# Low weight parts of the side-by-side steps made on GpSimd instead of stored and reloaded, weight sums moved, keys evacuated first, zero matmuls at the start

## The chip, the cores and the metric

The kernel runs on one core of one Trainium2 chip. The metric is the device time of one execution in microseconds (us); the median of three runs is given. TensorE is called PE, VectorE DVE, ScalarE ACT, GpSimd POOL; SyncE (SP) issues the DMAs.

## What is computed

One decoder layer on x of 2048 rows (tokens) by 2048 columns, in float32. One input projection feeds a convolution branch (1024 channels) and a sliding-window attention (16 heads of 64, 2 key/value heads); both are gated, joined and mapped by an output projection, and the result is added to the scaled input and normalized.

```python
proj = x @ w_in + b_in                       # 2048 x 2048 by 2048 x 5376
c_val, c_glu, c_gate, q, k, v, a_gate = split(proj)
h = causal_depthwise_conv(c_val * sigmoid(c_glu), width=31) + conv_b
y_conv = silu(layer_norm(h)) * silu(c_gate)
y_attn = window_attention_with_sinks(q, k, v) * silu(a_gate)
y = concat(y_conv, y_attn) @ w_out + b_out
out = layer_norm(2 ** 0.25 * x + y)
```

## The kernel before, in words

**Split products.** Every float32 matrix product is made of three matmuls. A matrix is split into a high part (rounded to the matmul's own type by a copy on ACT) and a low part (the rest: the matrix minus the high part, by `lo_part`, L134, one subtraction on DVE or POOL). `mm3` (L783) then adds high x high, high x low and low x high into one PSUM bank. A weight tile is 128 x 1024; its raw, high and low form (`wr`, `wh`, `wl`) have three buffers each.

**Steps.** The work is a list of steps (L664), one weight tile of 24 matmuls each. The input projection takes four chunks of 512 tokens, each of 52 steps (`PER`):

- eight `first` steps: four column tiles (k, v, one value and one gate tile of the convolution) side by side in four banks, each step adding two of the sixteen pieces of the inner dimension;
- 36 `in` steps: the 18 column tiles 4 to 21 one by one, two steps a tile. Beside them runs the attention of the chunk (`att_scores`, `att_transpose`, `att_values`, from step 13 of the chunk);
- eight `last` steps: the tiles 22 to 25 side by side, as in `first`.

Then the gates (`gate`) and the output projection (`out`) follow, both as Strassen products with seven products instead of eight, in eight steps each.

**Low parts of the weights.** In chunk 0 the low part of each of the 52 weight tiles is computed (on DVE for `first`, on POOL otherwise; `split_w`, L717) and stored to DRAM (`wlo`, L571, stored at L894). In chunks 1 to 3 `load_lo` (L711) loads it back two steps ahead; `has_lo` (L704) tells which steps have a stored low part.

**Weight sums.** The Strassen products need sums of weight quarters (`tsum`) and, for every other piece, stored low parts (`olo`). They are made in 32 jobs beside the projection: `tsum_load` (L580) loads four tiles of 128 x 512, `tsum_part` (L590) makes up to four subtractions (L598) and, for even pieces, seven high copies on ACT and seven low parts, on POOL, and queues their stores. Job j starts at step 10 + 6 j (L772).

**Background.** `run_bg` (L175) runs four or five pieces a step of the depthwise convolution on DVE (31 taps of 128 x 512 a tile, L234), or of its norm. The sums over channels (`csum`, L239, and `vsum`, L276) run on POOL.

**Evacuation.** At the end of the `first` steps `evac_in` (L377) empties four banks, in the order 2, 3, 1, 0 (L914): the two convolution tiles, v, then k. For k, the last block of the chunk before is first copied to the front of the key tiles (L390 and 391). The next step's tile takes the bank that k had.

**What sets the order.** All DMAs go through one queue on SP, in the order in which they are written (`dma`, L71). Each engine runs its instructions in one fixed order, made when the program is built, from priorities in the source's order and from modelled readiness; an instruction that waits holds back all behind it on its engine.

At the start (L851 to 866) the first weights and inputs are loaded and split, and PE begins when they are there.

Of the kernel before, what the change touches and what calls it, by code (L numbers as in the profile page):

```python
# [8 lines left out]
F32 = mybir.dt.float32  # L9
# [7 lines left out]
P = 128  # L17
# [11 lines left out]
NB = SC // P  # L29
KT = D // P  # L30
NSLOT = 69

PRODS = {"gate": (1, 2, 5, 6, 3, 7, 4), "out": (1, 2, 6, 5, 3, 7, 4)}

# [16 lines left out]
def hybrid_layer_kernel(ctx, tc, x, xT, w_first, w_in, w_out, consts, b_out, ln_g, ln_b, out):  # L51
# [79 lines left out]
    def copy(dst, src):  # L131
        A.activation(out=dst, in_=src, func=AF.Copy)  # L132
# [244 lines left out]
    def evac_in(c, t, kind, j, ps):  # L377
# [9 lines left out]
            store_later(hd[j][:, 30 + c * SC:30 + c * SC + SC], u)  # L387
            later.append((st["n"] + 3, lambda: cq.append((c, j))))
        elif kind == "k":
            for t in (*ks, *kl):  # L390
                copy(t[:, 0:P], t[:, 4 * P:5 * P].bitcast(F32))
            for kv in range(2):
                rows = slice(kv * HD, (kv + 1) * HD)
                for dst in (rows, slice((1 - kv) * HD, (2 - kv) * HD)):
# [3 lines left out]
        elif kind == "q":  # L398

            st["q", j] = [slot(f"q{kv}_{c}_{j}", F32R) for kv in range(2)]  # L400
            for kv in range(2):
                qs = st["q", j][kv]
                rows, other = slice(kv * HD, (kv + 1) * HD), slice((1 - kv) * HD, (2 - kv) * HD)
                A.activation(out=qs[rows], in_=ps[rows], func=AF.Identity, bias=b1[rows])
                V.scalar_tensor_tensor(out=qs[other], in0=ps[rows], scalar=b1[rows], in1=qs[rows].bitcast(F32),
                                       op0=ALU.add, op1=ALU.subtract)
        elif kind == "v":
            raw = slot(f"vraw{c}")
            A.activation(out=raw, in_=ps, func=AF.Identity, bias=b1)
            copy(vt[:, 0], vt[:, 4].bitcast(F32))  # L410
            pt = ps_pt.tile([P, 4, P], F32, tag="pt", name=f"vT{c}")
            for b in range(NB):
                T.transpose(out=pt[:, b, :], in_=raw[:, b * P:(b + 1) * P], identity=ident)
            for kv in range(2):
                src = pt[:, :, kv * HD:(kv + 1) * HD]
                hi, lo = vt[:, 1:5, kv, 0:HD], vt[:, 1:5, kv, HD:P]
                copy(hi, src)
                V.tensor_tensor(out=lo, in0=src, in1=hi.bitcast(F32), op=ALU.subtract)
# [130 lines left out]
    def gen_y(what, blk, i, k):  # L549
# [8 lines left out]
        if i == 5:  # L558
# [9 lines left out]
            for i in (5, 6, 7, 4) for q in pieces}  # L568
    olo = {(i, *q): dram.tile([P, 1024], F32, tag=f"O{i}_{q}", name=f"O{i}_{q[0]}{q[1]}_{q[2]}")
           for i in range(1, 8) for q in pieces if q[2] % 2 == 0}  # L570
    wlo = [dram.tile([P, 1024], F32, tag=f"wlo{n}", name=f"wlo{n}") for n in range(52)]  # L571

    def quarter(what, dp, p, a, b):

# [88 lines left out]
    PER = 52  # L663
# [38 lines left out]
                yield  # L702

    def has_lo(n):  # L704
        return n >= PER and (steps[n][0] not in strassen or steps[n][4] % 2 == 0)

    def lo_src(n):
        s = steps[n]
# [8 lines left out]
    def split_w(n, parts=1):  # L717
# [6 lines left out]
        for i in range(parts):  # L724
            w = slice(i * 1024 // parts, (i + 1) * 1024 // parts)
            copy(hi[:, w], t[:, w])
            if not has_lo(n):
                lo_part(G if steps[n][0] != "first" else V, lo[:, w], t[:, w], hi[:, w])
        los[n] = lo
        splits[n] = ((hi[:, 0:512], hi[:, 512:1024]), (lo[:, 0:512], lo[:, 512:1024]))  # L730

# [37 lines left out]
                    at(base + 47 + p, gen_y, *prods[0], k)  # L769
    for j in range(32):  # L770
        job = (("gate", "out")[j // 16], j // 8 % 2, j // 2 % 4, j % 2)
        n = 10 + 6 * j  # L772
        at(n, tsum_load, *job)
        for k, i in enumerate((1, 2, 3, 5, 7, 6, 4)):
            at(n + 2 + k // 2, tsum_part, *job, i)
# [72 lines left out]
            store(c, s, d)  # L848


    w0 = load_w(0, 2)  # L851
    load_x(0, 0)
    next(w0)
# [14 lines left out]
    for n, s in enumerate(steps):  # L868
# [20 lines left out]
        else:  # L889
            list(load_w(n + 3))  # L890
            load_lo(n + 2)
            split_w(n + 2)
        if n < PER:
            dma(out=wlo[n], in_=los[n].bitcast(F32))  # L894
        for f, *args in att.get(n, []):
            f(*args)
        if s[0] in ("first", "last"):
# [13 lines left out]
                        h, l = (w[t // 2][:, t % 2 * 256 + kk * P:t % 2 * 256 + kk * P + P] for w in (hi, lo))  # L911
                    mm3(st["acc"][t], h, l, xh, xl, k == 0, k == KT - 1)
            if p == 7 and s[0] == "first":
                for t in (2, 3, 1, 0):  # L914
                    evac_in(c, t, *ORDER[t], st["acc"][t])
            elif p == 7:
                for t in range(4):
                    evac_in(c, 22 + t, *ORDER[22 + t], st["acc"][t])
            run_bg(5)
        elif s[0] == "in":  # L920
            _, c, t, kind, j, hf = s
# [145 lines left out]
```

## Time and profile before

| | us |
|---|---|
| median of three runs (lowest, highest) | 2650.05 (2649.9, 2653.05) |
| the profiled execution | 2651.39 |
| its span, first to last instruction | 2649.7 |
| PE busy | 2547.9 (96%) |
| DVE busy | 2086.1 (79%) |
| ACT busy | 1303.0 (49%) |
| POOL busy | 972.9 (37%) |
| mean granted TensorE clock | 0.988 of full speed |

The profile lists what each engine did in one execution. "Busy" of PE is from modelled ends of matmuls, which overlap; the distance from one start to the next tells the pace. In the list of waits, a row such as `PE in L786 <- DMA wl<-wlo` says that the matmuls of line 786 on tile `in` waited for the DMA that loads `wl` from `wlo`, with the total, the number of times and the longest in us. A group row gives engine, operation, tiles, shapes and count, then busy us and mean ns, then the idle time before. A row of the timeline gives start and duration in us, and in brackets the idle time before and what ended it. A row of a window gives busy us and count of each engine, the granted clock, the DMA share and GB/s.

### The profile page before, as it was taken

What the parts mean: (1) busy time and instruction counts of PE and PEld (TensorE: products, weight loads), DVE (VectorE), ACT (ScalarE), POOL (GpSimd) and SP (SyncE); (2) the same over time, 40 slices, a digit from 0 to 9 for tenths busy, and PEclk for the clock granted to TensorE, in tenths of its full rate; (3) what the DMA queues carried; (4) which work ended last, traced back from release to release, by engine and by line L of the source; (5) the groups of instructions that cost most, each with busy time, mean ns of one, the idle gap of its engine ahead of it and who ended that gap; (6) DMA issues with size and microseconds to landing.
All of it is one profiled execution on the core that took longest, in us unless ns stands there. A gap on an engine that the chain in (4) does not pass through costs nothing.

```text
span 2649.7 us, 35489 instructions
## 1 busy us (share of the span) xinstructions
PE 2547.9 (96%) x11680; PEld 2108.7 (80%) x11680; DVE 2086.1 (79%) x3261; ACT 1303.0 (49%) x2461; POOL 972.9 (37%) x614
## 2 busy tenths in 40 slices
PE   8999989999899999999999999999999999999995
PEld 6788777887688887888887787888888888888884
DVE  3787798858887868889759999977775677987688
ACT  4577435776347765467535434544554323233321
POOL 2677824445144452426423222324222222212224
PEclk9999999999999999999999999999999999999997
DMA  7675898757986689966887767786888987899794
GB/s 278 217 260 193 287 326 277 243 177 262 339 299 249 203 296 350 328 226 224 272 274 248 246 236 268 268 292 216 292 289 289 327 304 267 305 357 341 276 319 156
DMA packets 331674, 720.43 MB, mean 272 GB/s; under 512 B 37857, under 2 KB 95329, under 8 KB 331489
## 3 DMA queue, kind: packets, MB, share of 16 engines
q1 hardware_dynamic: 331488, 718.16, 78.4%
q8 instruction: 92, 1.51, 0.2%
q14 instruction: 94, 0.76, 0.1%
HBM read 564.79 MB, written 153.21 MB: 271 GB/s over the span
## 4 chain that ended last, share of the span: by engine, by line
PE 60%; DVE 18%; DMA 9%; ACT 5%; issue 3%; POOL 2%; SPq 2%; DVEq 0%; ACTq 0%; POOLq 0%
PE in L786 6%; DVE cv L234 6%; PE in L785 6%; PE in L784 6%; PE out L785 3%; PE out L784 3%; PE out L786 3%; SPq L75 2%; PE gate_s L786 2%; PE gate_s L784 2%; PE gate_s L785 2%; DMA wl<-wlo 2%; PE out_s L784 2%; PE out_s L786 2%; PE out_s L785 2%
## 5 line engine op out<-in xcount | busy, mean ns | idle before, releaser
L135 POOL TENSOR_TENSOR wl<-wr,wh 128x1024 fp32r<-128x1024 f32 (+1 forms) x158 | 393.8, 2494 | 973.7 <-ACT wh L132 639.6
L132 ACT ACTIVATE wh<-wr 128x1024 fp32r<-128x1024 f32 (+1 forms) x436 | 455.0, 1046 | 546.5 <-DMA wr<-in_w_in_dram 81.4
L234 DVE SCALAR_TENSOR_TENSOR cv<-h,cst,cv 128x512 f32<-128x512 f32 x928 | 696.0, 752 | 18.8
L786 PE MATMUL in<-xh,wl 128*128 128x512 f32 x1280 | 502.1, 393 | 14.0 <-DMA wl<-wlo 14.0
L784 PE MATMUL in<-xh,wh 128*128 128x512 f32 x1280 | 504.1, 394 | 9.7 <-ACT xh L132 6.2
L785 PE MATMUL in<-xl,wh 128*128 128x512 f32 x1280 | 502.9, 393 | 0.0
L786 PEld LDWEIGHTS in<-xh,wl 128*128 128x128 f32 x1280 | 242.6, 190 | 67.6 <-DMA wl<-wlo 17.3
L784 PEld LDWEIGHTS in<-xh,wh 128*128 128x128 f32 x1280 | 242.5, 189 | 59.7 <-ACT xh L132 6.9
L785 PEld LDWEIGHTS in<-xl,wh 128*128 128x128 f32 x1280 | 242.4, 189 | 49.1 <-DVE xl L135 1.0
L785 PE MATMUL out<-wl,yhout 128*128 128x512 f32 x448 | 175.5, 392 | 6.4 <-DMA wl<-O_out 5.5
L132 ACT ACTIVATE yhout<-yrout 128x512 fp32r<-128x512 f32 x112 | 70.0, 627 | 216.3 <-DVE yrout L557 206.7
L786 PE MATMUL out<-wh,ylout 128*128 128x512 f32 x448 | 175.1, 391 | 0.0
L784 PE MATMUL out<-wh,yhout 128*128 128x512 f32 x448 | 166.9, 391 | 0.4 <-ACT wh L132 0.4
L135 POOL TENSOR_TENSOR plc<-pmc,phc 128x512 fp32r<-128x512 f32 x64 | 83.2, 1299 | 223.9 <-ACT phc L132 186.4
L135 DVE TENSOR_TENSOR ylgate<-yrgate,yhgate 128x512 fp32r<-128x512 f32 x112 | 109.7, 980 | 40.0 <-ACT yhgate L132 39.5
L135 DVE TENSOR_TENSOR ylout<-yrout,yhout 128x512 fp32r<-128x512 f32 x112 | 102.1, 912 | 45.0 <-ACT yhout L132 43.8
L322 ACT ACTIVATE pr<-pr,sm 128x128 f32<-128x128 f32 x256 | 99.6, 390 | 66.1 <-DVE sm L318 65.8
L132 ACT ACTIVATE yhgate<-yrgate 128x512 fp32r<-128x512 f32 x112 | 69.9, 625 | 115.3 <-DVE yrgate L557 93.9
L784 PE MATMUL gate_s<-yhgate,wh 128*128 128x512 f32 x304 | 119.0, 391 | 2.1 <-DVE g L451 1.9
L786 PE MATMUL gate_s<-yhgate,wl 128*128 128x512 f32 x304 | 119.1, 392 | 1.9 <-POOL wl L135 1.9
L785 PE MATMUL gate_s<-ylgate,wh 128*128 128x512 f32 x304 | 118.6, 390 | 0.0
L784 PE MATMUL gate<-yhgate,wh 128*128 128x512 f32 x288 | 112.8, 392 | 0.2 <-DVE g L451 0.2
(368 smaller groups left out, 5872.2 us busy)
## 6 DMA issues: line engine op xcount, KB each, us to landing
wl<-wlo SPq DMA_DIRECT2D x156, 512.0 KB, 5.1
wr<-in_w_in_dram SPq DMA_DIRECT2D x144, 512.0 KB, 5.9
yrout<-yd SPq DMA_DIRECT2D x192, 256.0 KB, 5.8
wr<-in_w_in_dram SPq DMA_DIRECT2D x320, 128.0 KB, 4.4
yrgate<-in_xT_dram SPq DMA_DIRECT2D x144, 256.0 KB, 5.1
wr<-T_gate SPq DMA_DIRECT2D x64, 512.0 KB, 6.3
wr<-T_out SPq DMA_DIRECT2D x61, 512.0 KB, 6.9
wl<-O_gate SPq DMA_DIRECT2D x56, 512.0 KB, 3.9
```

Source lines behind the costliest of these rows:

```text
L75: queue.append(nc.sync.dma_start(out=out, in_=in_).ins)
L132: A.activation(out=dst, in_=src, func=AF.Copy)
L135: eng.tensor_tensor(out=dst, in0=src, in1=hi.bitcast(F32), op=ALU.subtract)
L234: V.scalar_tensor_tensor(out=a if t == TAPS - 1 else acc, in0=x_, scalar=w, in1=acc, op0=ALU.mult, op1=ALU.add)
L322: A.activation(out=p3[:, u, :], in_=p3[:, u, :], func=AF.Exp, scale=HD ** -0.5, bias=sm[:, 1, u:u + 1], accum_out=sm[:, 3, u:u + 1])
L784: T.matmul(o, lh, mh, start=start, stop=False)
L785: T.matmul(o, lh, ml, start=False, stop=False)
L786: T.matmul(o, ll, mh, start=False, stop=stop)
```

## The change

- **Low parts.** Only the 36 `in` steps (8 to 43 of a chunk) keep stored low parts. In the `first` and `last` steps of chunks 1 to 3 the low part is computed on POOL from the raw tile and the high part. In chunk 0 the `first` steps still use DVE; the 16 side-by-side steps no longer store theirs.
- **Weight sums.** Jobs 0 to 7 stay where they were; in chunks 1 to 3 eight jobs a chunk start at steps 8, 12, 17, 21, 26, 30, 35 and 39 of the chunk.
- **Evacuation.** The order is 0, 1, 2, 3: k, v, then the convolution's tiles. The copies from the chunk before (keys and values) move from the evacuation to step 4 of the `first` steps.
- **Zero matmuls.** DVE clears one tile, and ten matmuls of it into a bank that is otherwise unused then stand ahead of everything on PE.

```diff
+WARM = 10
...
         elif kind == "k":
-            for t in (*ks, *kl):
-                copy(t[:, 0:P], t[:, 4 * P:5 * P].bitcast(F32))
...
             A.activation(out=raw, in_=ps, func=AF.Identity, bias=b1)
-            copy(vt[:, 0], vt[:, 4].bitcast(F32))
...
-    wlo = [dram.tile([P, 1024], F32, tag=f"wlo{n}", name=f"wlo{n}") for n in range(52)]
+    wlo = {n: dram.tile([P, 1024], F32, tag=f"wlo{n}", name=f"wlo{n}") for n in range(8, 44)}
...
     def has_lo(n):
-        return n >= PER and (steps[n][0] not in strassen or steps[n][4] % 2 == 0)
+        kind = steps[n][0]
+        return n >= PER if kind == "in" else kind in strassen and steps[n][4] % 2 == 0
...
             if not has_lo(n):
-                lo_part(G if steps[n][0] != "first" else V, lo[:, w], t[:, w], hi[:, w])
+                lo_part(V if n < 8 else G, lo[:, w], t[:, w], hi[:, w])
...
-        n = 10 + 6 * j
+        n = 10 + 6 * j if j < 8 else j // 8 * PER + 8 + j % 8 * 9 // 2
...
+    warm = slot("warm", F32R)
+    V.memset(warm.bitcast(F32), 0.0)
+    wps = right_banks("warm")[3]
+    for k in range(WARM):
+        T.matmul(wps, warm[:, 0:P], warm, start=k == 0, stop=k == WARM - 1)
...
-        if n < PER:
+        if n in wlo:
             dma(out=wlo[n], in_=los[n].bitcast(F32))
...
             if p == 7 and s[0] == "first":
-                for t in (2, 3, 1, 0):
+                for t in range(4):
                     evac_in(c, t, *ORDER[t], st["acc"][t])
...
+            if p == 4 and s[0] == "first":
+                for t in (*ks, *kl):
+                    copy(t[:, 0:P], t[:, 4 * P:5 * P].bitcast(F32))
+                copy(vt[:, 0], vt[:, 4].bitcast(F32))
```

## The prediction

> **What bounds the kernel now.** I read the page first, then busy time by stage, then the list of waits of PE.
>
> ```profile
> span 2649.7 us, 35489 instructions
> PE 2547.9 (96%) x11680; PEld 2108.7 (80%) x11680; DVE 2086.1 (79%) x3261; ACT 1303.0 (49%) x2461; POOL 972.9 (37%) x614
> ```
>
> PE is the bound, so only time in which PE stands still or runs slowly can be won. To see where that is, I counted 24 matmuls a step along PE, cut the projection where the eight side-by-side steps at a chunk's start and end begin and stop (192 matmuls), and asked for busy time between the cuts (busy us and count by engine, granted clock, DMA share, GB/s).
>
> ```profile
> core 0: us, PE busy (x) PEld busy (x) DVE busy (x) ACT busy (x) POOL busy (x), PEclk, DMA share, GB/s
> 0.00:56.20 56.20, 48.02 (x192) 37.94 (x192) 22.34 (x31) 26.85 (x40) 9.42 (x22) 1.00 0.79 276
> 56.20:304.10 247.90, 238.67 (x1188) 201.45 (x1189) 174.82 (x308) 153.92 (x382) 185.68 (x115) 0.99 0.71 236
> 304.10:348.40 44.30, 43.88 (x194) 35.90 (x193) 41.99 (x56) 14.59 (x19) 31.31 (x18) 1.00 0.91 311
> 348.40:403.50 55.10, 47.08 (x194) 37.28 (x192) 52.53 (x72) 19.56 (x25) 9.22 (x6) 0.94 0.91 309
> 403.50:659.10 255.60, 242.21 (x1193) 202.99 (x1194) 197.41 (x367) 174.36 (x414) 124.14 (x94) 0.98 0.70 239
> 659.10:710.00 50.90, 46.23 (x193) 36.87 (x192) 36.72 (x50) 14.40 (x18) 11.84 (x9) 0.97 0.98 334
> 710.00:757.90 47.90, 44.61 (x194) 35.67 (x192) 41.48 (x59) 22.57 (x31) 15.14 (x12) 1.00 0.86 315
> 757.90:997.20 239.30, 235.84 (x1191) 199.61 (x1192) 186.25 (x355) 158.62 (x390) 114.07 (x89) 1.00 0.74 259
> 997.20:1041.20 44.00, 44.00 (x196) 36.40 (x195) 39.04 (x63) 24.96 (x35) 5.97 (x5) 1.00 1.00 338
> 1041.20:1090.30 49.10, 45.78 (x193) 36.91 (x192) 41.33 (x59) 24.04 (x35) 26.20 (x20) 0.97 0.99 365
> 1330.10:1374.20 44.10, 44.10 (x196) 36.46 (x196) 30.46 (x42) 16.57 (x23) 3.68 (x2) 1.00 0.83 276
> ```
>
> The same 192 matmuls take 44.00 us where nothing is waited for (997.2 to 1041.2). I take that as the floor of such a stage. Over it lie 11.1 us in the first steps of chunk 1, 6.9 in its last steps, 3.9 in the first of chunk 2, 0 in its last, 5.1 in the first of chunk 3 and 0.1 in its last: **27.1 us in the six stages that lose their loads of low parts**. Their DMA share is 0.83 to 1.00, that of the long single-tile stages 0.70 to 0.74. The waits say what it is:
>
> ```profile
> PE in L786 <- DMA wl<-wlo: 14.0, 7, 3.6
> PE in1l_s L786 <- DMA wl<-wlo: 4.7, 4, 3.0
> PE in L784 <- DVE kl L396: 3.5, 4, 2.0
> PE gate_s L786 <- POOL wl L135: 1.9, 1, 1.9
> PE vT L413 <- ACT vraw L409: 1.4, 1, 1.4
> PE in0l_s L786 <- POOL wl L135: 0.4, 1, 0.4
> ```
>
> Eleven waits for a stored low part make 18.7 us (columns: total, times, longest). Much of the rest is a slow clock behind a wait:
>
> ```profile
> 669.30:672.70 3.40, 3.40 (x9) 2.65 (x8) 3.22 (x6) 0.00 (x0) 0.00 (x0) 0.51 1.07 389
> 1495.40:1498.80 3.40, 3.40 (x9) 2.32 (x8) 2.67 (x5) 3.30 (x7) 0.00 (x0) 0.50 0.92 311
> ```
>
> At a granted clock of 0.51, 9 matmuls ran where 15 fit at the 0.227 us that a matmul takes at full clock (below). That is 1.4 us a stretch.
>
> **The change part by part.**
>
> *Low parts by POOL.* 48 loads and 16 stores go, out of these:
>
> ```profile
> wl<-wlo SPq DMA_DIRECT2D x156, 512.0 KB, 5.1
> wlo<-wl SPq DMA_DIRECT2D x52, 512.0 KB, 5.8
> L135 POOL TENSOR_TENSOR wl<-wr,wh 128x1024 fp32r<-128x1024 f32 x154 | 387.4, 2516 | 971.4 <-ACT wh L132 637.3 <-DMA wr<-in_w_in_dram 100.8 <-DMA wl<-O_out 62.6
> L598 POOL TENSOR_TENSOR tbgate<-tbgate,tbgate 128x512 f32<-128x512 f32 x64 | 86.0, 1344 | 58.4 <-DMA tbgate<-in_w_in_dram 51.7 <-PE in L786 3.8
> L135 POOL TENSOR_TENSOR tlgate<-tbgate,thgate 128x512 fp32r<-128x512 f32 x56 | 74.5, 1339 | 52.1 <-ACT thgate L132 39.2 <-DMA O_gate<-tlgate 12.8
> ```
>
> POOL gets 48 subtractions of 2.52 us, one per step of 44.0/8 = 5.5 us, so it is busy 46% of these stages with them. They lie beside matmuls. What is late next is the raw weights, ACT's copy, then POOL. The raw buffer is now held until POOL has read it, and SP's load of the next one, with all loads queued behind it on SP, waits for that. The last steps of chunk 0 already work so, with weight sums on POOL besides (31.3 us of 44.3). They are 0.3 us over the floor, with 0.4 us of waits for POOL. From the 27.1 us I deduct 0.5 us a stage for such waits (3.0). I deduct 2.5 us for DVE: in 304.1 to 403.5 it has 94.5 us of work, and if all of it must stay there, the first stage of chunk 1 cannot go below 94.5 - 44.3 = 50.2 us (6.2 over the floor, the upper bound; none if the surplus moves on to the next stage, where DVE has 197.4 of 255.6). Third, a collision of POOL with DVE:
>
> ```profile
> 1414.41 7.66 POOL L135 TENSOR_TENSOR wl<-wr,wh 128x1024 fp32r<-128x1024 f32 x1 [6.95 <-DMA wr<-in_w_in_dram]
> 1415.51 3.69 DVE L293 TENSOR_TENSOR conv<-conv,rstd 128x512 f32<-128x512 f32 x6
> ```
>
> Beside a train of DVE operations on two SBUF tiles, one low part took 7.66 us instead of 2.52. Such trains (the convolution's norm) reach into some of the six stages. What a late low part costs PE is seen in the gate stage: a wait of 1.9 us and a slow stretch of 1.4, together 3.3. I take one such event (bounds none and six, 0 to 20 us). **Gain of this part: 27.1 - 3.0 - 2.5 - 3.3 = 18.3 us; bounds 25.3 (0.3 us a stage left) and, with all three at their worst, -2.**
>
> The Trainium skill (GPSIMD Engine Reference, Key points) says that POOL shares its SBUF interfaces with VectorE and contends with DVE instructions that have two SBUF inputs, and sends elementwise work to VectorE. The stretched row agrees; taken as frequent it is the third rival below.
>
> *Weight sums beside single tiles only.* In chunks 1 to 3, eight jobs instead of six fall into each long stage. A job is 4 subtractions and, every other pair of jobs, 7 low parts: 4 x 1.34 + half of 7 x 1.34 = 10 us of POOL on average, so 20 us more per stage. The loads and stores move with them on SP. Between chunk 2's long stage (POOL 114.1, 239.3 us) and chunk 0's (185.7, 247.9) a stage grew by 8.6 us for 71.6 us of POOL, 0.12 a us; that gives 2.4 us a stage, 7.2 in all, if POOL is the reason, and nothing if it isn't. I take **4 us lost**.
>
> *Keys and values first.* The order of each engine's instructions is made when the program is built, from readiness, so the source's order binds little:
>
> ```profile
> 50.22 0.68 ACT L395 ACTIVATE ks<-in,cst 64x512 fp32r<-64x512 f32 x1 [5.97 <-PE in L786]
> 55.34 0.76 DVE L396 SCALAR_TENSOR_TENSOR kl<-in,cst,ks 64x512 fp32r<-64x512 f32 x1 [1.94 <-ACT ks L395]
> 56.24 0.47 PE L784 MATMUL in<-xh,wh 128*128 128x512 f32 x1 [1.98 <-DVE kl L396]
> ```
>
> The key's evacuation already begins as its tile is done and still ends at 56.1. So of the 3.5 us of waits for `kl` I take 0.6 as won, and the 1.4 us for `vraw`, which no longer stands behind two other evacuations: **2.0 us** (0 to 4.9). The five copies at step 4 fall into ACT's idle time (5.97 us before 50.22); uncovered they would cost about 1.4 us.
>
> *Zero matmuls.*
>
> ```profile
> 6.03 0.80 PE L784 MATMUL in<-xh,wh 128*128 128x512 f32 x1 [6.03 <-ACT xh L132]
> 9.05 0.80 PE L785 MATMUL in<-xl,wh 128*128 128x512 f32 x1
> 13.91 0.43 PE L784 MATMUL in_s<-xh,wh 128*128 128x512 f32 x1
> 19.65 0.39 PE L785 MATMUL in_s<-xl,wh 128*128 128x512 f32 x1
> 20.78 0.39 PE L784 MATMUL in_s<-xh,wh 128*128 128x512 f32 x1
> ```
>
> From 9.05 to 13.91 lie 11 starts at 0.44 us, from 19.65 to 20.78 five at 0.226. PE starts at half speed 6 us into the span. Ten zero matmuls at 0.44 us fill 4.4 of those 6 us, in which PE idles. Were the clock full from 9.05 on, the eleven would take 2.5 us: 2.4 won. If the clock doesn't come earlier, nothing; if their end passes 6.03, up to 0.5 lost. I take **1.8**.
>
> The Trainium skill (TensorE: Matmul & The Clock Gate, Part 1) puts the warm-up at about 3.4 us of sustained matmuls in a free-running window. This trace took 7.9 us, with gaps. By the skill the zeros alone release the clock, and the gain is the upper end, 2.4.
>
> *Sum.* 18.3 - 4 + 2.0 + 1.8 = 18.1 us. The profiled execution took 2651.4 us (its span 2649.7 and 1.7 around it), so 2633.3; it lies 1.3 above the median of the runs, 2650.05, which gives **2632**.
>
> **The rivals.**
>
> *POOL's queue blocks (slower).* POOL works in order, and the convolution's sums wait there for DVE:
>
> ```profile
> 226.28 1.29 POOL L239 TENSOR_TENSOR csum<-conv,conv 128x512 f32<-128x512 f32 x1 [1.67 <-DVE conv L234]
> 732.38 1.29 POOL L239 TENSOR_TENSOR csum<-csum,conv 128x512 f32<-128x512 f32 x1 [26.92 <-DVE conv L234]
> 1356.12 1.29 POOL L239 TENSOR_TENSOR csum<-csum,conv 128x512 f32<-128x512 f32 x1 [36.62 <-DVE conv L234]
> ```
>
> The second and third lie in side-by-side steps. Today nobody needs POOL there. If a low part is queued behind such a sum, PE waits as soon as the wait passes the lead of two steps, 11 us: 15.9 and 25.6, together 41.5 us, against 18.1 won: 2673. For it: DVE is 95% busy in the worst stage. Against it: in chunk 0, where POOL makes a low part in every step, a sum waited 1.67 us.
>
> *The long stages fill up.* If chunks 2 and 3 come to chunk 0's 247.9 us, that is 2 x 8.6 = 17.2 us in place of the 4 taken: 2645. For it, POOL and ACT at 75% and 62% in chunk 0; against it, chunk 0 carries 36 low parts that these stages load.
>
> *POOL and DVE collide often.* Six events of 3.3 us instead of one: 2632 + 16.5 = 2648.5. For it, the 7.66 us row; against it, chunk 0's last steps, with POOL 71% busy and splits of x on DVE, 0.3 us over the floor.
>
> *All goes well.* Only 0.3 us a stage stay, and the long stages don't grow: 25.3 + 2.4 + 3.4 = 31 us, 2619; with a third of what chunk 1's long stage lies over chunk 2's (16.3 us), 2613.
>
> **How the numbers follow.** Forecast 0.54; all well 0.2; full stages and collisions 0.14 together, of which 0.10 end within 0.2% (5.3 us, about what a measurement tells from no change); queue blocked 0.12. Faster by over 0.2%, which is below 2644.7: 0.54 + 0.2 + 0.04 = 0.78; same 0.10; slower 0.12. The range goes from 2612 (all well) to 2650 (the two rivals without a gain) and leaves the blocked queue out.
>
> **What would show it.** Right: the first and last stages of chunks 1 to 3 at 44 to 48 us; no wait for `wlo` there; POOL's low parts about 2.5 us; matmuls at 0.23 us before 10 us; the long stages within 3 us of before. Wrong: PE waiting for POOL's `wl` by more than 8 us in these stages, behind `csum` or a stretched subtraction; long stages over 250 us; matmuls at 0.43 us until 13.9 as before.

## The result and the profile after

The changed kernel takes **2666.8 us** (median of four runs, 2664.95 to 2668.04) against 2651.6 us for the kernel before on the same chip: ratio 1.0061, 95% interval 1.0049 to 1.0073. It is 0.6% slower, where a gain of 0.7% was forecast. The profiled execution took 2664.95 us. Its page:

```profile
span 2663.2 us, 35501 instructions
PE 2554.0 (96%) x11690; PEld 2115.6 (79%) x11690; DVE 2132.3 (80%) x3262; ACT 1303.2 (49%) x2461; POOL 1096.6 (41%) x662
```

POOL's 48 subtractions are there (48 more instructions). DVE is busy 46 us longer with one instruction more: its operations have become longer. PE does the same work in a longer span, so it stands still or runs slowly more. Busy time by stage, cut as in the prediction (busy us and count for PE, PEld, DVE, ACT, POOL, then granted clock, DMA share, GB/s):

```profile
0.00:52.30 52.30, 49.36 (x207) 39.93 (x207) 22.04 (x31) 25.78 (x39) 9.42 (x22) 1.00 0.63 217
341.70:392.10 50.40, 47.22 (x198) 38.17 (x196) 49.00 (x65) 16.68 (x22) 24.94 (x13) 0.93 0.59 199
392.10:661.10 269.00, 247.20 (x1190) 205.86 (x1189) 216.82 (x379) 175.04 (x413) 140.74 (x104) 0.95 0.73 245
661.10:704.70 43.60, 43.60 (x194) 36.08 (x194) 42.44 (x60) 18.01 (x25) 21.63 (x10) 1.00 0.80 258
704.70:748.50 43.80, 43.80 (x196) 36.26 (x195) 38.80 (x52) 14.85 (x19) 15.68 (x7) 1.00 0.42 138
748.50:995.50 247.00, 239.05 (x1190) 201.09 (x1189) 190.81 (x350) 161.63 (x395) 133.92 (x103) 0.99 0.76 260
995.50:1047.10 51.60, 46.22 (x195) 37.38 (x194) 45.18 (x54) 25.13 (x35) 26.99 (x11) 0.97 0.56 185
1047.10:1102.10 55.00, 46.14 (x197) 37.17 (x196) 51.28 (x72) 17.61 (x24) 18.55 (x8) 0.94 0.51 168
```

Four things happened at once. The start is shorter (52.3 us to the end of the first stage, 56.2 before). Chunk 1's last stage and chunk 2's first now run at the floor of 44 us. Chunk 2's last stage, which had nothing to lose its loads for (44.0 us before), takes 51.6, and chunk 3's first 55.0 instead of 49.1, although the DMA share in them has fallen from 1.00 and 0.99 to 0.56 and 0.51. And the long stage of chunk 1 takes 269.0 us instead of 255.6. PE's list of waits names the new ones:

```profile
PE in L786 <- POOL wl L136: 8.8, 3, 4.8
PE in2l_s L786 <- POOL wl L136: 5.4, 2, 3.9
PE var L257 <- ACT vs0h L133: 5.1, 1, 5.1
PE in L786 <- DMA wl<-wlo: 4.3, 1, 4.3
```

None of the waits for `wlo` in the side-by-side steps is left; the one in the list (4.3 us) lies in chunk 1's long stage, at 620.3 us. Waits for POOL's low part make 14.2 us instead.

**How a low part on POOL comes late.** The wait of 3.9 us lies in the last step of chunk 2's last stage. Followed back through the timelines of the changed kernel, first POOL:

```profile
1012.90 2.49 POOL L136 TENSOR_TENSOR wl<-wr,wh 128x1024 fp32r<-128x1024 f32 x1 [4.05 <-DMA wr<-in_w_in_dram]
1016.87 2.40 POOL L136 TENSOR_TENSOR wl<-wr,wh 128x1024 fp32r<-128x1024 f32 x1 [1.48 <-ACT wh L133]
1020.72 2.56 POOL L136 TENSOR_TENSOR wl<-wr,wh 128x1024 fp32r<-128x1024 f32 x1 [1.44 <-DMA wr<-in_w_in_dram]
1035.10 5.20 POOL L136 TENSOR_TENSOR wl<-wr,wh 128x1024 fp32r<-128x1024 f32 x1 [11.82 <-ACT wh L133]
```

and DVE at the same moments:

```profile
1013.06 2.62 DVE L150 TENSOR_SCALAR nt<-nt 128x512 f32<-128x512 f32 x1
1017.52 2.31 DVE L148 TENSOR_TENSOR nt<-v,rstd 128x512 f32<-128x512 f32 x1
1020.95 2.88 DVE L136 TENSOR_TENSOR xl<-xr,xh 128x512 fp32r<-128x512 f32 x1
1033.19 0.69 DVE L163 SCALAR_TENSOR_TENSOR cn_0u<-cn_0t,cn_0u 128x512 f32<-128x512 f32 x1
```

Each of the first three DVE operations starts within a low part on POOL and ends 0.3 to 0.6 us after it (1015.68 against 1015.39, 1019.83 against 1019.27, 1023.83 against 1023.28). Together they take 6.0 us longer than these forms take when nothing holds them (0.41, 0.68 and 0.69 us). In the kernel before, the first of these forms takes 0.41 us there, and the norm's first output `cn_0u` is done 32.1 us into the stage instead of 38.4:

```profile
1018.07 0.41 DVE L149 TENSOR_SCALAR nt<-nt 128x512 f32<-128x512 f32 x1
1028.60 0.68 DVE L162 SCALAR_TENSOR_TENSOR cn_0u<-cn_0t,cn_0u 128x512 f32<-128x512 f32 x1
```

This lateness reaches PE by way of ACT, which also works in order. After:

```profile
1031.50 0.82 ACT L158 ACTIVATE cn_0u<-conv,half 128x512 f32<-128x512 f32 x1 [10.86 <-DVE conv L294]
1033.97 1.05 ACT L133 ACTIVATE wh<-wr 128x1024 fp32r<-128x1024 f32 x1
```

ACT stands 10.86 us before the norm's first activation, whose data DVE makes late. The high copy of the stage's last weight tile is queued behind it. That tile had landed at 1023.1 us, and POOL needs the copy for its low part (the wait of 11.82 us above). In the kernel before, the same copy stands just ahead of the norm's first activation (1025.17 and 1026.14 us). The last row of POOL above then took 5.20 us beside DVE's train of `conv` times `rstd`, and PE waited:

```profile
1035.60 1.89 DVE L294 TENSOR_TENSOR conv<-conv,rstd 128x512 f32<-128x512 f32 x3
1040.35 0.50 PE L786 MATMUL in2l_s<-xh,wl 128*128 128x512 f32 x1 [3.86 <-POOL wl L136]
```

SP stood 11.5 us behind the store of `cn_0u` as well, but in this stage that cost PE nothing: the weights behind it landed at 1038.0 us, and the step that uses them began at 1053.8 us without a wait.

So the two engines hold each other up. The DVE groups of these two stages show it on the whole (count, then busy us and mean ns), first of the changed kernel, then of the one before:

```profile
L235 DVE SCALAR_TENSOR_TENSOR cv<-h,cst,cv 128x512 f32<-128x512 f32 x69 | 49.7, 751 | 0.7
L136 DVE TENSOR_TENSOR xl<-xr,xh 128x512 fp32r<-128x512 f32 x16 | 16.2, 1014 | 0.9 <-ACT xh L133 0.9
```

```profile
L234 DVE SCALAR_TENSOR_TENSOR cv<-h,cst,cv 128x512 f32<-128x512 f32 x63 | 47.4, 752 | 1.3
L135 DVE TENSOR_TENSOR xl<-xr,xh 128x512 fp32r<-128x512 f32 x16 | 11.7, 735 | 0.0
```

`xl`, with both inputs in SBUF, went from 735 to 1014 ns. The taps `cv`, with one input in PSUM, stayed at 751. The Trainium skill (GPSIMD Engine Reference, Key points) names two kinds of DVE instructions that contend: those with two SBUF inputs, as `xl` has, and those in a two-port performance mode; whether the one-input form of 0.41 us runs in such a mode the trace doesn't say. Another page of the Trainium skill (Trainium Architecture — The Big Picture, What this means for kernel authors) calls it an exclusive lock, not a shared bandwidth; DVE's ends just behind POOL's agree with that.

In the first stages of chunks 1 and 3 the queue of POOL itself also blocks:

```profile
369.38 1.27 POOL L240 TENSOR_TENSOR csum<-csum,conv 128x512 f32<-128x512 f32 x1 [5.24 <-DVE conv L235]
370.62 7.00 POOL L136 TENSOR_TENSOR wl<-wr,wh 128x1024 fp32r<-128x1024 f32 x3
1075.32 1.26 POOL L240 TENSOR_TENSOR csum<-conv,conv 128x512 f32<-128x512 f32 x1 [12.86 <-DVE conv L235]
1076.55 7.02 POOL L136 TENSOR_TENSOR wl<-wr,wh 128x1024 fp32r<-128x1024 f32 x3
```

Each time three low parts stood behind a sum that waited for DVE, and PE waited for the first of them, 3.1 and 4.75 us: 7.8 of the 14.2 us. In chunk 3's first stage SP's queue does carry the lateness, in the same step:

```profile
1065.87 1.59 SPq L76 DMA_DIRECT2D hd<-gu  x2
1067.56 1.35 SPq L76 DMA_DIRECT2D wr<-in_w_first_dram  x3
```

SP waited 9.2 us for `gu`, which DVE makes. The weights behind that store landed at 1072.2 us, and PE waited 3.2 us for their high copy.

### The profile page after: what moved, and what is told of

It is laid out like the page before. It is cut to its first block, busy times and chain, and to the rows that moved or that the text cites. A ratio compares the mean times of both kernels' runs of the same rounds, so it can differ in the third digit from the quotient of the medians.

```text
span 2663.2 us, 35501 instructions
## 1 busy us (share of the span) xinstructions
PE 2554.0 (96%) x11690; PEld 2115.6 (79%) x11690; DVE 2132.3 (80%) x3262; ACT 1303.2 (49%) x2461; POOL 1096.6 (41%) x662
## 4 chain that ended last, share of the span: by engine, by line
PE 39%; DVE 10%; DMA 3%; issue 1%; ACT 1%; SPq 0%; POOL 0%; DVEq 0%; ACTq 0%; POOLq 0%
PE out L785 3%; PE out L786 3%; PE out L784 3%; DVE cv L235 3%; PE out_s L785 2%; PE out_s L786 2%; PE out_s L784 2%; PE gate_s L786 2%; PE gate_s L784 2%; PE gate_s L785 2%; PE gate L784 1%; PE gate L786 1%; PE gate L785 1%; PE gate_v L784 1%; PE gate_t L786 1%
## 5 line engine op out<-in xcount | busy, mean ns | idle before, releaser
L136 POOL TENSOR_TENSOR wl<-wr,wh 128x1024 fp32r<-128x1024 f32 (+1 forms) x206 | 515.6, 2505 | 1068.3 <-ACT wh L133 792.4
L235 DVE SCALAR_TENSOR_TENSOR cv<-h,cst,cv 128x512 f32<-128x512 f32 x928 | 690.6, 751 | 16.5
L785 PEld LDWEIGHTS in<-xl,wh 128*128 128x128 f32 x1280 | 243.3, 190 | 48.4
## 6 DMA issues: line engine op xcount, KB each, us to landing
yrout<-yd SPq DMA_DIRECT2D x192, 256.0 KB, 5.9
yrgate<-in_xT_dram SPq DMA_DIRECT2D x144, 256.0 KB, 4.9
```

Of the source, the lines that this page charges most:

```text
L136: eng.tensor_tensor(out=dst, in0=src, in1=hi.bitcast(F32), op=ALU.subtract)
L235: V.scalar_tensor_tensor(out=a if t == TAPS - 1 else acc, in0=x_, scalar=w, in1=acc, op0=ALU.mult, op1=ALU.add)
L785: T.matmul(o, lh, ml, start=False, stop=False)
```

## The experiments

The table gives the stages in us (24 matmuls counted a step along PE; "first" and "last" are the side-by-side stages, "long" the single tiles). They come from one profiled execution of each kernel, which lay up to 9.6 us from the median of its runs.

| stage | before | after | sums only | low parts only | start and evacuation | halves |
|---|---|---|---|---|---|---|
| chunk 0 first | 50.2 | 46.3 | 51.0 | 50.0 | 46.9 | 46.0 |
| chunk 1 first | 55.1 | 50.3 | 55.9 | 52.5 | 55.1 | 43.9 |
| chunk 1 long | 255.6 | 269.1 | 268.4 | 256.0 | 250.5 | 251.3 |
| chunk 1 last | 51.0 | 43.5 | 43.5 | 43.5 | 51.7 | 43.8 |
| chunk 2 first | 47.9 | 43.9 | 44.2 | 55.0 | 47.5 | 47.9 |
| chunk 2 long | 239.3 | 247.0 | 245.0 | 239.8 | 240.2 | 239.0 |
| chunk 2 last | 44.0 | 51.6 | 44.0 | 54.1 | 44.0 | 51.9 |
| chunk 3 first | 49.1 | 55.0 | 48.4 | 65.1 | 47.8 | 58.6 |
| chunk 3 long | 239.8 | 244.4 | 245.2 | 239.1 | 237.6 | 239.1 |

The kernel before, run beside each group, had medians of 2650.4 (first four runs), 2647.8 (next four), 2650.9, 2648.3 and 2646.5 us. A ratio is against the runs of before beside it.

### Which part costs what

**Sums at the old places** (the changed kernel otherwise):

```diff
-        n = 10 + 6 * j if j < 8 else j // 8 * PER + 8 + j % 8 * 9 // 2
+        n = 10 + 6 * j
```

> The changed kernel with the weight sums at their old places (job j at step 10 + 6 j), all else as changed. Theory A (the sums packed beside single tiles cost the 25.6 us by which the long stages of chunks 1 to 3 grew: 255.6, 239.3 and 239.8 us before, 269.1, 247.0 and 244.4 after; the low parts on POOL are a gain): the long stages fall back to within 3 us of before and the time to 2641 to 2646 us. Theory B (the low parts on POOL are the loss: POOL's operations stretch DVE's, DVE falls behind, and its backlog and the stores that wait for it fill the long stages too; where the sums stand matters little): 2660 us or more, with long stages still over 250, 245 and 243 us.

Measured: 2660.2 us, ratio 1.0036 [1.0027, 1.0046]. The long stages of chunks 1 to 3 take 251.5, 238.6 and 238.5 us, no longer than before, and a loss stays. Chunk 2's first stage takes 54.1 us, against 43.9 in the changed kernel: at their old places the sums stand on POOL beside the low parts there.

**Sums only** (the kernel before with the line above the other way round):

> The kernel before with the weight sums alone moved. Theory A: the long stages grow as in the changed kernel (some 25 us), the side-by-side stages, relieved of the sums' transfers, win a part of their 27 us over the floor: 2660 to 2675 us. Theory B: no more than 3 us of growth in the long stages, 2640 to 2652 us.

Measured: 2662.9 us, 1.0043 [1.0027, 1.0058]. The sums run nothing on DVE, yet at least 184 of its 3261 instructions and 162 of ACT's 2461 stand elsewhere in their order than before. What the sums cost by themselves and by the new order these runs don't separate.

**Low parts only** (the kernel before with the change's lines for `wlo`, `has_lo` and `split_w`):

> The kernel before with the low parts of the side-by-side steps on POOL and not stored, nothing else. Theory A: the side-by-side stages win as in the changed kernel or better, the long ones stay: 2630 to 2645 us. Theory B: 2660 us or more; PE waits for POOL's low parts in the last steps of chunk 2 and the first of chunk 3 as after the whole change (11 us there).

Measured: 2666.9 us, 1.0059 [1.0041, 1.0077].

**Start and evacuation only** (the zero matmuls, the order 0 to 3, the moved copies):

> The kernel before with the zero matmuls and the new evacuation order (with the moved copies) alone. Both theories: the first stage of chunk 0 ends about 4 us earlier as in the changed kernel, and the long stage of chunk 0 stays within 2 us: 2644 to 2648 us. If the order made at build time shifts more than the two edits, it shows here as a change of more than 6 us in chunks 1 to 3.

Measured: 2638.7 us, 0.9955 [0.9934, 0.9977], more than expected. Chunks 1 to 3 took 7.5 us less, 5.1 of them in chunk 1's long stage. By what was written down before the run, that points to a shift in the order made at build time beside the two edits.

The parts add up: +12.5 for the sums, +16.5 for the low parts, -11.7 for start and evacuation make +17.3, against +15.2 for the whole (2666.8 - 2651.6), with 4 to 6 us of uncertainty in each part. Two of the parts lose, and the only gain is the one with the smaller forecast. By stage, the low parts alone won 10.0 us in chunk 1 (first and last) and lost 33.2 in chunk 2's first and last and chunk 3's first (7.1, 10.1 and 16.0).

### The low parts

**POOL's low parts in chunk 1 alone**, beside the new start and evacuation; chunks 2 and 3 load stored ones:

```diff
-        return n >= PER and (steps[n][0] not in strassen or steps[n][4] % 2 == 0)
+        if kind in strassen:
+            return steps[n][4] % 2 == 0
+        return n >= 2 * PER or n >= PER and kind == "in"
```

> Zero matmuls and evacuation order as changed, weight sums at their old places, low parts on POOL only in chunk 1's side-by-side steps; chunks 2 and 3 load stored ones as before. Theory C (low parts on POOL win where the convolution's norm is not at work on DVE, chunk 1, and lose where it is, the last steps of chunk 2 and the first of chunk 3): chunk 1's first and last steps at 47.6 and 43.8 us as in e1, the others as in e4: 2638.7 - 7.4 - 7.9 = 2623, 2618 to 2628 us. Theory D (POOL's low parts push a loss into whatever follows them): 2635 us or more, the loss in chunk 2.

Measured: 2635.6 us, 0.9958 [0.9939, 0.9976]. Chunk 1's last stage takes 44.9 us (51.0 before), chunks 2 and 3 are within 2.2 us a stage of the start and evacuation alone: the loss of the low parts lies in chunks 2 and 3. Chunk 1's first stage stayed at 54.2 where 47.6 was expected, and on the whole the ratio isn't distinct from that of the start and evacuation alone.

**Stores later** (the kernel with the sums at the old places; stores of `hd` and of the normed rows three steps later, the convolution's queue too):

```diff
-            store_later(hd[j][:, 30 + c * SC:30 + c * SC + SC], u)
-            later.append((st["n"] + 3, lambda: cq.append((c, j))))
+            store_later(hd[j][:, 30 + c * SC:30 + c * SC + SC], u, 5)
+            later.append((st["n"] + 6, lambda: cq.append((c, j))))
...
-                store_later(od[c, 8 + j], u, 3)
+                store_later(od[c, 8 + j], u, 6)
```

> e1 (low parts on POOL in all side-by-side steps, sums at their old places) with the stores of the convolution's inputs and outputs three steps later on SP's queue, and the convolution's loads of them too. Theory C, its second half (SP's queue holds the weights' loads behind stores that wait for DVE, 9 to 12 us at a time): the last steps of chunk 2 and the first of chunk 3, 54.7 and 63.1 us in e1, fall to 44 to 50 each, the time to 2635 to 2645 us. Theory D (POOL itself is late: raw weights, copy, subtraction and the sums before it): no less than 50 and 58 us there, 2652 to 2662 us.

Measured: 2683.4 us, 1.0137 [1.0116, 1.0159]. It shifted the whole convolution and gave new stalls in the long stage of chunk 1 (264.0 us against 251.5) and in the gates (645.6 against 628.6). Chunk 2's last and chunk 3's first stage together fell from 117.7 to 110.6 us. Too much moved at once for it to tell SP's queue apart.

**Halves** (sums at the old places; each low part of a side-by-side step as two operations of half the columns):

```diff
-                lo_part(V if n < 8 else G, lo[:, w], t[:, w], hi[:, w])
+                for h in range(2) if n >= PER and steps[n][0] in ("first", "last") else ():
+                    v = slice(h * 512, h * 512 + 512)
+                    lo_part(G, lo[:, v], t[:, v], hi[:, v])
+                if n < PER or steps[n][0] not in ("first", "last"):
+                    lo_part(V if n < 8 else G, lo[:, w], t[:, w], hi[:, w])
```

> e1 with each low part of a side-by-side step of chunks 1 to 3 made in two halves of 128x512 on POOL (about 1.3 us each instead of 2.4). If DVE's lag comes from waiting for a whole operation of POOL, a collision costs half: DVE's busy time in the last steps of chunk 2 and the first of chunk 3 falls by several us and the two stages by 5 us or more of their 117.7, the time to 2645 to 2655 us. If the collisions don't matter: 2658 to 2663 us, stages unchanged.

Measured: 2640.5 us, 0.9974 [0.9956, 0.9991], 19.8 us less than with whole low parts, or 17.2 when each is taken against the runs of before beside it. Four stages fell, together by 17.2 us as well: chunk 1 first, chunk 2 first and last, and chunk 3 first. With halves:

```profile
342.70:386.60 43.90, 43.90 (x198) 36.33 (x196) 43.40 (x61) 14.92 (x19) 25.74 (x19) 1.00 0.67 217
681.60:729.50 47.90, 44.50 (x198) 36.21 (x196) 42.41 (x58) 21.79 (x32) 33.93 (x26) 1.00 0.58 197
968.50:1020.50 52.00, 46.66 (x196) 37.33 (x195) 44.26 (x56) 22.29 (x31) 34.31 (x23) 0.97 0.63 204
1020.50:1079.00 58.50, 49.83 (x196) 37.47 (x195) 57.22 (x73) 26.81 (x41) 48.92 (x36) 0.94 0.72 240
```

and with whole ones:

```profile
343.20:390.90 47.70, 44.56 (x198) 36.23 (x197) 47.20 (x63) 15.22 (x20) 24.92 (x13) 1.00 0.67 218
686.20:740.30 54.10, 46.70 (x196) 37.21 (x195) 46.75 (x60) 20.56 (x29) 33.07 (x20) 0.94 0.51 177
979.00:1033.60 54.60, 47.87 (x195) 38.22 (x194) 47.77 (x56) 24.64 (x35) 31.04 (x15) 0.91 0.59 194
1033.60:1096.70 63.10, 49.56 (x197) 39.17 (x196) 60.17 (x73) 24.78 (x37) 46.39 (x27) 0.86 0.66 224
```

POOL does the same work in 0.8 to 3.3 us more; DVE's busy time falls by 3 to 4 us a stage (47.20 to 43.40, 47.77 to 44.26), and PE's clock and stage follow. A new order made at build time is not the reason: in the two traces all instructions of ACT and DVE (2461 and 3262) stand in the same order by operation and tile, and those of POOL too but for the halves. But TensorE could also start a step on the first half, so:

**Halves in the opposite order** (the columns that PE reads first are made last):

```diff
-                for h in range(2) if n >= PER and steps[n][0] in ("first", "last") else ():
+                for h in (1, 0) if n >= PER and steps[n][0] in ("first", "last") else ():
```

> The kernel with halved low parts that gave 2640.5 us (sums at the old places), with the two halves made in the opposite order, the columns that TensorE reads first being made last: TensorE can't start a step any earlier than with a whole low part. Theory (short operations on POOL and VectorE get in each other's way for a shorter time): 2639 to 2645 us. Rival (the gain of 20 us was TensorE starting on the first half while the second was being made): 2655 to 2661 us, as with whole low parts.

Measured: 2642.9 us, 0.9976 [0.9963, 0.9988], the same. The gain doesn't come from an earlier start; it is the length of POOL's operation, in which DVE is held. Halves don't cure it all: chunk 2's last stage and chunk 3's first still take 17.4 us more than before, and ACT still stands 13.4 us at `cn_0u` in the former. Against the start and evacuation alone (0.9955) even halved low parts are no gain.

**The normed rows' stores later** (halves, with the line of the stores alone changed from 3 to 5 steps):

```diff
-                store_later(od[c, 8 + j], u, 3)
+                store_later(od[c, 8 + j], u, 5)
```

> The kernel with halved low parts that gave 2640.5 us, with the stores of the convolution's normed rows issued five steps after their making instead of three; nothing else is changed. In the last stage of chunk 2 SP stood 9.6 us behind the first of these stores, whose data VectorE makes late. Theory (SP's queue: the weight loads behind that store come late): the last stage of chunk 2 falls from 51.9 us to 46 to 48, the first of chunk 3 from 58.6 to 50 to 55, the time to 2628 to 2636 us. Rival (low parts come late from POOL whatever SP does): both stages within 2 us, 2638 to 2643 us.

Measured: 2648.2 us, ratio 0.9991 [0.9977, 1.0006], no better than the halves. Chunk 2's last stage takes 53.1 us, chunk 3's first 55.1. SP no longer stands at `cn_0u`; its longest waits in the two stages are those for `gu`, 21.3 us in three. The store of `cn_0u` is out of the way, and chunk 2's last stage is no shorter. ACT is where it was:

```profile
1009.51 0.82 ACT L158 ACTIVATE cn_0u<-conv,half 128x512 f32<-128x512 f32 x1 [13.38 <-DVE conv L294]
1011.46 1.04 ACT L133 ACTIVATE wh<-wr 128x1024 fp32r<-128x1024 f32 x1
```

The weights of that copy had landed at 998.8 us, and PE waited 3.4 us for the low part made from it. So SP's store was not what held PE in this stage. A kernel with the copy ahead of the norm's activation in ACT's order was not run.

### The sums

**The norm's matmul later** (sums only, and the variance's matmul queued six steps after the split instead of three):

```diff
-                    later.append((st["n"] + 3, lambda: conv_var(c)))
+                    later.append((st["n"] + 6, lambda: conv_var(c)))
```

> e2 (weight sums alone moved) with the matmuls that sum up the convolution's variance, and what follows them, three steps later. Theory E (the packed sums delay POOL's and ACT's chain to the variance, PE stands 7.0 us at the variance's first matmul and runs slowly behind it): chunk 1's long stage falls from 268.4 to 257 to 262 us, the time to 2650 to 2656. Rival (the packed sums cost by making every step of the attention later, wherever PE waits): the wait moves to the attention's matmuls, the stage stays at 266 us or more, and the time at 2660 or more.

Measured: 2671.8 us, 1.0089 [1.0071, 1.0107]. PE's wait for `vs0h` stayed (6.9 us): the order made at build time put that matmul in the same place on PE (the later chunks' moved by three steps). So this run doesn't tell what the wait is worth. How it arises, in the kernel with the sums only (ACT, then POOL, then PE):

```profile
575.36 0.63 ACT L271 ACTIVATE sq<-conv 128x512 f32<-128x512 f32 x1 [1.37 <-POOL vsum L276]
576.06 1.26 POOL L276 TENSOR_TENSOR vsum<-vsum,sq 128x512 f32<-128x512 f32 x1 [0.74 <-ACT sq L271]
580.04 0.79 PE L256 MATMUL var<-vs0h,ones 128*128 128x512 f32 x1 [6.96 <-ACT vs0h L132]
```

and in the kernel before:

```profile
565.24 2.18 ACT L271 ACTIVATE sq<-conv 128x512 f32<-128x512 f32 x4
```

Before, ACT makes the last four squares in one train, and `vs0h` is ready at 572.5 us, 8.3 us before PE reads it at 580.8. With the sums packed, each square waits for POOL's sum and each sum for the square: 2.0 us a pair, in lockstep, until PE stands. Each square and each sum takes a slot, so a shortage of slots would do this; the rows name only who released whom.

**Sums in halves** (sums only, POOL's subtractions and low parts of the sums as two of 128x256):

```diff
-            G.tensor_tensor(out=t, in0=ab[0], in1=ab[1], op=ALU.subtract)
+            for h in range(2):
+                v = slice(h * 256, h * 256 + 256)
+                G.tensor_tensor(out=t[:, v], in0=ab[0][:, v], in1=ab[1][:, v], op=ALU.subtract)
```

> The kernel before with the new places of the weight sums, and each of the sums' operations on POOL (subtraction and low part, 128x512) split into two of 128x256. The same values and the same work. Collision theory (POOL's long operations hold up VectorE's operations on two SBUF inputs, and are held up by them, so that the convolution's norm beside the dense sums comes late): 2650 to 2658 us instead of the 2662.9 that the new places alone gave, and the long stage of chunk 1 falls from 268 us to 260 or less. Rival (SP's queue, or the number of sums a step, whatever their grain): 2661 to 2667 us and that stage stays at 266 to 270.

Measured: 2690.4 us, 1.0151 [1.0129, 1.0173]. Neither theory had this. Chunk 0's long stage, and the long stage of chunk 1:

```profile
56.70:316.20 259.50, 243.07 (x1188) 204.81 (x1189) 184.31 (x308) 153.82 (x382) 190.62 (x161) 0.97 0.68 228
425.90:695.60 269.70, 246.26 (x1192) 204.27 (x1193) 202.81 (x369) 175.35 (x414) 148.52 (x162) 0.96 0.73 245
```

In chunk 1 DVE's busy time falls by 6.6 us (209.45 with whole operations), and the stage stays as long: there the grain isn't the cause. In chunk 0, where POOL is busiest, the stage grows by 11.8 us and the next by 11.6. The order on ACT and DVE is the same there in both runs. Why 46 more operations and 5 us more of POOL cost so much there stays open.

**Halves in both places** (the changed kernel with the two edits):

> The changed kernel whole, with POOL's operations halved in both places: the low parts of the side-by-side steps of chunks 1 to 3 (two of 128x512) and the sums' subtractions and low parts (two of 128x256). If the grain is the cause in both, the loss against the kernel before is gone: 2636 to 2650 us instead of 2666.8. If it is the cause for the low parts alone: 2648 to 2656. If neither: 2662 us or more.

Measured: 2691.8 us, 1.0151 [1.0127, 1.0175]. Chunk 0 loses as in the run above (262.6 and 55.1 us), which hides what the low parts win (chunk 1 first 45.6).

**Sums away from the norm**, and denser:

```diff
-        n = 10 + 6 * j
+        n = 10 + 6 * j if j < 8 else j // 8 * PER + (7, 10, 13, 16, 19, 22, 38, 41)[j % 8]
```

> The kernel before with the sums of chunks 1 to 3 at offsets 7, 10, 13, 16, 19, 22, 38 and 41 of their chunk instead of every four and a half steps from 8: denser, but away from the steps 26 to 37 in which the norm of the convolution of the chunk before runs. Place theory (norm and sums at the same steps): the long stage of chunk 1 falls from the 268.4 us of the even spacing to 262 or less, the time from 2662.9 to 2645 to 2656 us. Density theory (sums in flight hold slots and queues): that stage is 268 us or more, the time 2662 to 2680.

Measured: 2662.7 us, 1.0055 [1.0033, 1.0076]. The long stage of chunk 1 takes 264.4 us, between the two theories: the wait for the variance is gone, and PE waits 8.9 us for attention's `phc` instead. In these two placements the place of the sums decides which wait it is, not that there is one.

**Three slots fewer** (the kernel before, `NSLOT` 69 to 66, nothing else):

> The kernel before with 66 slots instead of 69 and nothing else changed. Sums every 4.5 steps instead of 6 hold some three slots more. Density theory (slots are short): the long stage of chunk 1 grows from 255.6 us to 262 or more, the time to 2658 to 2680 us. Place theory (slots are not what is short): that stage within 2.5 us, the time 2648 to 2656.

Measured: 2671.3 us, 1.0087 [1.0066, 1.0108]. The long stages grow by 6.4, 7.2 and 3.5 us, with the same operations on POOL (124.4 us in chunk 1's, 124.1 before).

So three slots fewer cost the kernel before about as much as the denser sums. With the slots the order made at build time changes a little too (at least 64 of ACT's 2461 instructions and 92 of DVE's 3261 stand elsewhere). That the denser sums cost what they do for want of slots is not shown by this.

**One slot more** for the sums only:

```diff
-NSLOT = 69
+NSLOT = 70
...
-        o = small.tile([P, 2, P], F32, tag="o", name=f"o{c}_{r}_{b}")
+        o = small.tile([P, 2, P], F32, tag="o", name=f"o{c}_{r}_{b}", bufs=3)
```

> The kernel before with the new places of the sums (2662.9 us) and 70 slots instead of 69; the room comes from the small tile that attention's values pass through, three buffers instead of four. Slot theory (the denser sums run short of slots, and three fewer cost 20.9 us, 7 us each): 2652 to 2659 us, and the long stage of chunk 1 falls from 268.4 us to 260 to 266. Rival (it is the density of operations on ACT, POOL and SP's queue): 2660 to 2666 us, that stage 266 to 270.

Measured: 2656.9 us, 1.0037 [1.0019, 1.0054]; the ratio isn't distinct from 1.0043. The three long stages fall by 1.6, 1.4 and 2.5 us (266.7, 243.6 and 242.7). Slots may be a part of it; how large a part, against the density of operations on ACT, POOL and SP, stays open.

### A faster version

**Halves in chunk 1 alone** (the kernel "POOL's low parts in chunk 1 alone" with the edit of the halves):

> The kernel before with the zero matmuls, the new order of evacuation and the moved copies, low parts by POOL in the side-by-side steps of chunk 1 alone, each in two halves of 128x512; the side-by-side steps of chunks 2 and 3 load stored low parts, and the sums stay at the old places. A candidate for the fastest: with whole low parts it gave 2635.6 us, of which the first stage of chunk 1 kept 54.2 us. Theory (the grain of POOL's operations): that stage falls to 44 to 48 us, the time to 2624 to 2632. Rival (the gain of the halves hangs on the stages of chunks 2 and 3, or the chunk 0 stores decide in chunk 1): 2634 to 2638 us.

Measured: 2630.1 us, 0.9926 [0.9905, 0.9948]. Chunk 1's first stage kept 53.1 us, so the time came without the stage that was to give it.

**The last steps' low parts stored from chunk 1:**

```diff
-        if n < PER:
-            dma(out=wlo[n], in_=los[n].bitcast(F32))
+        if n < 44 or 96 <= n < 104:
+            dma(out=wlo[n % PER], in_=los[n].bitcast(F32))
```

> The fastest kernel so far (2630.1 us: halves of low parts on POOL in chunk 1, stored ones in chunks 2 and 3), with the low parts of the last eight steps stored from chunk 1 instead of chunk 0. Theory (the stores of chunk 0's last stage stand ahead of the loads for chunk 1's first, which took 53.1 us against 43.9 without them): that stage falls to 44 to 48 us, the first of chunk 2 rises by less than that, and the time is 2622 to 2628 us. Rival (the same backlog is passed to chunk 2's first stage, 49.1 us now): 2628 to 2633 us.

Measured: 2626.5 us, 0.9913 [0.9889, 0.9937]. The first stages of chunks 1 and 2:

```profile
343.50:387.70 44.20, 44.20 (x198) 36.31 (x196) 43.70 (x62) 14.94 (x19) 25.23 (x19) 1.00 0.66 211
685.10:739.30 54.20, 47.53 (x195) 38.47 (x196) 43.08 (x61) 24.45 (x34) 15.19 (x12) 0.91 0.91 324
```

The first fell by 8.9 us, the second rose by 5.1: stores of a last stage stand ahead of the next chunk's loads, in either place.

**The same with one slot more:**

> The fastest kernel so far (2626.5 us, sums at the old places) with 70 slots instead of 69, the room taken as in the run beside it. Slot theory (the old places are short of slots too, 7 us each by the kernel with three fewer): 2615 to 2623 us. Rival (69 are enough at the old places): 2624 to 2630 us.

Measured: 2623.3 us, 0.9918 [0.9902, 0.9934], not distinct from the run before. Both are 0.8 to 0.9% faster than the kernel before.

## Why the prediction was wrong

- **Low parts by POOL: forecast 18.3 us won, measured alone 16.5 lost, outside the bounds.** The step that failed is "I take one such event (bounds none and six, 0 to 20 us)". It priced a stretched operation on POOL, seen once in the gate stage. It left out the other direction, DVE held for a whole low part (2.62 us instead of 0.41). In chunk 2's last stage that happened three times in a row and made the norm late by 6 us; ACT's and POOL's own order, and SP's queue in chunk 3's first stage, then carried the delay to the low parts and weights. In place of 3.3 us, the low parts alone lost 33.2 us in three stages. What held: the waits for `wlo` there went, an undisturbed low part takes 2.40 to 2.56 us, and in the changed kernel two stages came to the floor. What the sum also missed is that chunk 2's last stage stood at 44.0 us, with nothing to win and a norm on DVE to disturb: +7.6 us there, +5.9 in chunk 3's first. The stage it took as its model, chunk 0's last, has no norm beside it: the first variance comes at 580.8 us.
- **DVE as a bound of chunk 1's first stage: the step fell.** "Cannot go below 94.5 - 44.3 = 50.2 us" was the worst case, and 50.4 came out; but with halves the stage took 43.9 us with 43.4 us of DVE. So it was no bound, and 50.4 is luck: stretched operations filled that stage, and part of the work could move on.
- **Sums: forecast 4 us lost, measured 12.5.** The slope "0.12 a us" of POOL failed. It came from two stages with the same spacing of jobs. At the closer spacing the three long stages grew by 12.8, 5.7 and 5.4 us, and 7.4 and 3.7 were won back in the side-by-side stages beside. The sum has neither the tile slots, of which three fewer cost the kernel before about 23 us (2671.3 - 2648.3), nor the new order of the instructions. Which of these makes the 12.5 us stays open.
- **Zero matmuls and evacuation: forecast 3.8 us won, measured 11.7.** The zeros did what was forecast. After, PE is at full pace from 6.77 us on (the fourth row is 0.23 us behind the third):

```profile
1.51 0.79 PE L855 MATMUL warm_v<-warm 128*128 128x512 f32 x1 [1.51 <-DVE warm L852]
5.95 0.98 PE L784 MATMUL in<-xh,wh 128*128 128x512 f32 x2
6.77 0.40 PE L784 MATMUL in_s<-xh,wh 128*128 128x512 f32 x1
7.00 0.40 PE L785 MATMUL in<-xl,wh 128*128 128x512 f32 x1
```

  The stage's last matmul starts 2.2 us earlier (51.67 against 53.88 us), where 1.8 and at most 2.4 were forecast. The Trainium skill (TensorE: Matmul & The Clock Gate, Part 1) let the zeros alone release the clock; the rows agree. Another 1.8 us came at the evacuation behind it: the next step starts 0.58 us later instead of 2.36. Neither `kl` nor `vraw` is in PE's list of waits any more, so their 3.5 and 1.4 us all went, where 2.0 were taken. The rest was not foreseen: chunk 1's long stage fell from 255.6 to 250.5 us with the new order and the moved copies, and it is 250 to 253 us in every kernel that has them with the sums at the old places, but for the one with all stores later. Which of the two edits does it, or the order made at build time, stays open.
- **The rivals.** "POOL and DVE collide often" was the right mechanism with too small a price: it counted PE's waits for a slow POOL, and ended at 2648.5. "POOL's queue blocks" came true twice, in chunk 1's first stage and in chunk 3's (7.8 us on PE together), not in the two places and not with the 41.5 us that it named. "The long stages fill up" was right, and larger than its 17.2 us for chunks 2 and 3 by way of chunk 1. They came together, and each had been given its chance alone.
- **Small slips.** One of the eleven waits for `wlo` (1.5 us, at 942.5 us) lies in chunk 2's long stage, not in the six stages. The 3.4 us for keys and values under "All goes well" are not worked out anywhere. Neither changes the forecast.

## What to carry to other kernels

Before work is given to an idle engine, ask whom its operations hold while they run, not only whether it has time: here a 2.5 us subtraction on POOL held DVE's 0.4 us steps, and cutting it in two won some 17 us without a change in the work. Then ask what stands behind the engine that is held: on ACT, POOL and SP, which work in order, an instruction that waited for DVE held back weights that were ready or could have been loaded. A stage that already runs at its floor can only lose by such a change; leave it alone, as the faster version here does, and move the rest.

## What was not expected of the hardware

- DVE's short one-input operation (0.41 us) was held as long as the two-input ones: 2.62 us beside a low part on POOL. The taps with an input in PSUM kept their time (928 `cv` operations, none over 0.76 us, while the longest of 64 `xl` took 2.88), and so did a reduction of one SBUF tile (`sm<-pr`, 64 of them, none over 0.69 us).
- The holding goes both ways: POOL's low part took 5.20 us beside a train of two-input operations on DVE, and 2.40 to 2.56 beside single ones.
- With 128x256 operations on POOL instead of 128x512, chunk 0's two stages took 23 us more (259.5 and 55.2 us against 247.7 and 43.6), so a finer grain on POOL isn't always better.
